# Rotary embedding, split halves: three in-place slabs of four batches in place of five of two

## The chip, the cores and the metric

One core of one Trainium2 chip. The metric is the device time of one execution in microseconds (us), of which the profiled span (first to last instruction) is about 1.8 us less. The kernel before takes 163.34 us (median of four runs, 163.23 to 163.87). Runs are marked fast or slow; a run counts as slow when it is over 1.5% above the fastest run of the same kernel in the same session.

Names used below: PE (TensorE) does the matmuls, DVE (VectorE) and ACT (ScalarE) work element by element, POOL is GpSimd, SP (SyncE) here only issues DMAs. SBUF is the on-chip memory, PSUM the memory that PE writes. A cast here turns float32 into bf16; an eviction copies a result from PSUM to SBUF.

## The reference, cut to what matters

```python
batch, seq, dim, num_heads = 16, 512, 1024, 16     # x is float32, 33.6 MB
x = x.reshape(batch, seq, num_heads, 64)
x1, x2 = x[..., :32], x[..., 32:]
# cos, sin: [512, 32] float32, the same for every batch and head
rotated = np.concatenate([x1 * cos - x2 * sin,
                          x1 * sin + x2 * cos], axis=-1)      # float32, 33.6 MB
```

## The kernel before

The input is cut into eight slabs of two batches (4.2 MB). A slab is [128 partitions, 8192 floats]: each partition holds eight consecutive sequence positions, so that a DMA moves 128 rows of 32 KB. Results overwrite the slab in place, and the slab is stored from there. Five slabs fit; load 5 takes the buffer of slab 0 and waits until store 0 has landed.

```python
nb, slots, lead, rows = 2, 5, 5, 2          # cut: shapes
def load(s):
    slab[s] = slabs.tile([P, W], f32, tag="slab", name="slab")
    nc.sync.dma_start(out=slab[s], in_=dram(x, s))          # issued from SP
for s in range(lead): load(s)
# cut: cos and sin go by 64 rows of 1 KB into SBUF and by matmul to all partitions
for s in range(nslabs):
    xs = slab.pop(s)
    for k in range(rpp // rows):
        xk = view(xs, k * PW, (1, PW))                      # 2048 columns
        nc.scalar.copy(out=xb, in_=xk)                      # ACT: cast to bf16
        nc.vector.tensor_mul(out=t1, in0=xb, in1=tab(cc))   # DVE: two products
        nc.vector.tensor_mul(out=t2, in0=xb, in1=tab(ss))
        # cut: per bank of 512, PE adds t1 and the half-swapped t2 (identity weights)
        nc.scalar.copy(out=xk, in_=acc)                     # ACT: eviction, in place
    nc.scalar.dma_start(out=dram(out_flat, s), in_=xs)      # store, issued from ACT
    if s + lead < nslabs: load(s + lead)
```

A scheduler orders each engine's instructions when the kernel is built, so that the order on an engine is not the order of this text. It places casts of the next slab ahead of the last evictions and of the store of the current one.

Of the kernel before, what the change touches and what calls it, by code (L numbers as in the profile page):

```python
# [2 lines left out]

# [4 lines left out]


@with_exitstack  # L10
def kernel(
    ctx: ExitStack,
    tc: tile.TileContext,
    x: bass.AP,
    cos: bass.AP,
    sin: bass.AP,
    num_heads: int,
    out: bass.AP,
):
    nc = tc.nc  # L20
    P = nc.NUM_PARTITIONS

    batch, seq, dim = x.shape
    nh = num_heads
    hd = dim // nh
    half = hd // 2
    bf16 = mybir.dt.bfloat16
    f32 = mybir.dt.float32

    nb = 2  # L30
    slots = 5
    lead = 5
    nslabs = batch // nb
    rpp = nb * seq // P
    W = rpp * dim
    SP = seq // rpp
    rows = 2
    PW = rows * dim
    BANK = 512
    hpb = BANK // hd  # L40

    out_flat = out.rearrange("b s h d -> b s (h d)")

    singles = ctx.enter_context(tc.tile_pool(name="singles", bufs=1))
    slabs = ctx.enter_context(tc.tile_pool(name="slabs", bufs=slots))
    tpool = ctx.enter_context(tc.tile_pool(name="tpool", bufs=3))
    psum = ctx.enter_context(tc.tile_pool(
        name="psum", bufs=2, space=bass.MemoryType.PSUM))


    def dram(t, s):
        return bass.AP(tensor=t.tensor, offset=t.offset + s * nb * seq * dim,
                       ap=[[W, P], [1, W]])


    def view(t, offset, *dims):
        return dataclasses.replace(t, offset=t.offset + offset,
                                   ap=[t.ap[0], *[list(d) for d in dims]])


    slab = {}


    def load(s):
        slab[s] = slabs.tile([P, W], f32, tag="slab", name="slab")
        nc.sync.dma_start(out=slab[s], in_=dram(x, s))


    for s in range(lead):
        load(s)  # L70



    cos_sb = singles.tile([SP, rpp * half], f32, tag="cos_sb")
    sin_sb = singles.tile([SP, rpp * half], f32, tag="sin_sb")
    for t, src in ((cos_sb, cos), (sin_sb, sin)):
        nc.scalar.dma_start(out=t, in_=bass.AP(  # L77
            tensor=src.tensor, offset=src.offset,
            ap=[[rpp * half, SP], [1, rpp * half]]))

    ident = singles.tile([P, P], bf16, tag="ident")
    masks.make_identity(nc, ident)
    spread = singles.tile([SP, P], bf16, tag="spread")
    for g in range(P // SP):
        nc.gpsimd.tensor_copy(out=spread[:, g * SP:(g + 1) * SP],  # L85
                              in_=ident[:SP, :SP])


    cc1 = singles.tile([SP, rpp * hd], bf16, tag="cc1")
    ss1 = singles.tile([SP, rpp * hd], bf16, tag="ss1")  # L90
    nc.vector.tensor_copy(  # L91
        out=cc1, in_=view(cos_sb, 0, (half, rpp), (0, 2), (1, half)))
    sin_rows = view(sin_sb, 0, (half, rpp), (1, half))
    nc.vector.tensor_copy(  # L94
        out=view(ss1, 0, (hd, rpp), (1, half)), in_=sin_rows)
    nc.vector.tensor_scalar_mul(  # L96
        out=view(ss1, half, (hd, rpp), (1, half)), in0=sin_rows, scalar1=-1.0)
    cc = singles.tile([P, rpp * hd], bf16, tag="cc")
    ss = singles.tile([P, rpp * hd], bf16, tag="ss")
    for wide, one in ((cc, cc1), (ss, ss1)):  # L100
        acc = psum.tile([P, PW], f32, tag="acc", name="acc")
        for q in range(0, rpp * hd, BANK):
            n = min(BANK, rpp * hd - q)
            nc.tensor.matmul(view(acc, q, (1, n)), spread, view(one, q, (1, n)),  # L104
                             start=True, stop=True)
        nc.vector.tensor_copy(out=wide, in_=view(acc, 0, (1, rpp * hd)))  # L106

    for s in range(nslabs):
        xs = slab.pop(s)
        for k in range(rpp // rows):  # L110
            xk = view(xs, k * PW, (1, PW))
            xb = tpool.tile([P, PW], bf16, tag="xb")
            t1 = tpool.tile([P, PW], bf16, tag="t1")
            t2 = tpool.tile([P, PW], bf16, tag="t2")
            nc.scalar.copy(out=xb, in_=xk)  # L115

            def tab(t):
                return view(t, k * rows * hd, (hd, rows), (0, nh), (1, hd))

            nc.vector.tensor_mul(out=t1, in0=xb, in1=tab(cc))  # L120
            nc.vector.tensor_mul(out=t2, in0=xb, in1=tab(ss))  # L121
            acc = psum.tile([P, PW], f32, tag="acc")
            for q in range(0, PW, BANK):
                bank = view(acc, q, (1, BANK))
                nc.tensor.matmul(bank, ident, view(t1, q, (1, BANK)),  # L125
                                 start=True, stop=False)
                nc.tensor.matmul(  # L127
                    bank, ident,
                    view(t2, q + half, (hd, hpb), (-half, 2), (1, half)),
                    start=False, stop=True)  # L130

            nc.scalar.copy(out=xk, in_=acc)  # L132
        nc.scalar.dma_start(out=dram(out_flat, s), in_=xs)
        if s + lead < nslabs:
            load(s + lead)


# [1 line left out]
_INS = ['x', 'cos', 'sin', 'num_heads']  # L139
_OUTS = [((16, 512, 16, 64), 'float32')]  # L140

_NUMBERS = {'num_heads': 16}


# [26 lines left out]
```

## Time and profile before

| | kernel before |
|---|---|
| time, us | 163.34 |
| span of the profiled run, us | 161.5 |
| DMA packet time (two queues' shares x span), us | 97.3% x 161.5 = 157.1 |
| busy: ACT, PE, DVE, us | 117.2, 79.1, 76.4 |

From the page of the kernel before: the span; busy time by engine; the busy tenths and rate of DMA in 40 slices; the queues (q1 loads, q10 stores and tables; the last number is the share of 16 engines' span that their packets took); the costliest groups (operation, out<-in, count, busy us, mean ns); and the DMA issues.

```profile
span 161.5 us, 816 instructions
PE 79.1 (49%) x258; PEld 28.6 (18%) x258; DVE 76.4 (47%) x69; ACT 117.2 (73%) x65; POOL 1.1 (1%) x8
...
DMA  7999999999999999999999999999999999997996
...
q1 hardware_dynamic: 1152, 33.55, 48.9%
q10 hardware_dynamic: 1312, 33.69, 48.4%
...
L115 ACT CAST xb<-slab 128x2048 bf16<-128x2048 f32 x32 | 59.6, 1905 | 19.1 <-DMA slab<-in_x_dram 16.6
L120 DVE TENSOR_TENSOR t<-xb,cc 128x2048 bf16<-128x2048 bf16 x32 | 39.1, 1222 | 51.5 <-ACT xb L115 51.5
...
slab<-in_x_dram SPq DMA_DIRECT2D x8, 4096.0 KB, 29.6
out_dram<-slab ACTq DMA_DIRECT2D x8, 4096.0 KB, 25.5
```

The row of DMA digits says it all: nearly every slice is 9. The engines' waits (ACT is idle for 44 of 161.5 us) cost nothing while DMA has queued work. The one soft spot is near the end. From the windows view of the same kernel (stretch and its length in us; busy time and instruction count of PE, PE's weight loads, DVE, ACT and POOL; granted clock; DMA share; GB/s):

```profile
147.00:148.00 1.00, 0.43 (x3) 0.00 (x0) 0.00 (x0) 1.00 (x2) 0.00 (x0) 1.00 1.14 492
148.00:149.00 1.00, 0.00 (x0) 0.00 (x0) 0.00 (x0) 1.00 (x1) 0.00 (x0) 1.00 0.23 98
149.00:150.00 1.00, 0.00 (x0) 0.00 (x0) 0.00 (x0) 0.43 (x1) 0.00 (x0) 1.00 0.08 33
150.00:151.00 1.00, 0.00 (x0) 0.00 (x0) 0.00 (x0) 0.00 (x0) 0.00 (x0) 1.00 1.22 524
```

Here the queued stores are done and the last slab's own store waits for its last eviction. A packet is put down to the stretch in which it starts, so that the rate is rough. By the trace's DMA records (start, duration and size of each packet), at least half of the 16 engines are idle from 149.0 to 150.4 us, and at no other time between 1.9 us and the last packets at 160.1 us for longer than 0.5 us.

### The profile page before, as it was taken

How to read it: one execution, taken by the hardware profiler on the slowest of the kernel's cores; microseconds unless marked ns; L12 is line 12 of the kernel's file. 1: busy time of each engine (PE TensorE's matmuls, PEld its weight loads, DVE VectorE, ACT ScalarE, POOL GpSimd, SP SyncE). 2: the span in 40 equal slices, each digit the busy share in tenths (PEclk: the TensorE clock that was granted, in tenths of full speed). 3: DMA queues.
4: the chain of work that ended last, by engine and by line, in shares of the span. 5: the costliest groups of instructions: out<-in, count | busy, mean ns of one | idle time of the engine just before them, and what ended most of it. 6: DMA issues, size and time to landing. Idle time of an engine off the chain costs nothing.

```text
span 161.5 us, 816 instructions
## 1 busy us (share of the span) xinstructions
PE 79.1 (49%) x258; PEld 28.6 (18%) x258; DVE 76.4 (47%) x69; ACT 117.2 (73%) x65; POOL 1.1 (1%) x8
## 2 busy tenths in 40 slices
PE   0001189646069754932995288079754278085000
PEld 0000023212013221310341033023321022021000
DVE  0000699065099429707955484299335172280000
ACT  3006647994999999899989998969990697918000
POOL 2000000000000000000000000000000000000000
PEclk9999999999858998796599969957999557659855
DMA  7999999999999999999999999999999999997996
GB/s 260 398 398 406 422 487 389 414 495 389 389 503 406 389 495 410 389 503 406 391 495 406 400 487 414 398 479 422 398 479 418 389 487 422 398 479 316 389 389 260
DMA packets 2468, 67.29 MB, mean 417 GB/s; under 512 B 288, under 2 KB 416, under 8 KB 416
## 3 DMA queue, kind: packets, MB, share of 16 engines
q1 hardware_dynamic: 1152, 33.55, 48.9%
q10 hardware_dynamic: 1312, 33.69, 48.4%
q8 instruction: 2, 0.03, 0.1%
q14 instruction: 2, 0.02, 0.0%
HBM read 33.69 MB, written 33.55 MB: 416 GB/s over the span
## 4 chain that ended last, share of the span: by engine, by line
DMA 46%; PE 17%; ACT 14%; issue 9%; DVE 6%; ACTq 0%; DVEq 0%; SPq 0%
DMA out_dram<-slab 18%; DMA slab<-in_x_dram 18%; DMA sin_sb<-in_sin_dram 10%; PE acc L127 9%; ACT slab L132 8%; PE acc L125 7%; ACT xb L115 6%; DVE t L121 5%; DVE t L120 1%; PE acc L104 0%; ACTq L77 0%; DVE ss L94 0%; DVE ss L96 0%; DVEq L120 0%; ACTq L132 0%
## 5 line engine op out<-in xcount | busy, mean ns | idle before, releaser
L125 PE MATMUL acc<-t,ident 128*128 128x512 bf16 x128 | 58.8, 459 | 43.6 <-DVE t L120 33.3
L115 ACT CAST xb<-slab 128x2048 bf16<-128x2048 f32 x32 | 59.6, 1905 | 19.1 <-DMA slab<-in_x_dram 16.6
L132 ACT COPY slab<-acc 128x2048 f32<-128x2048 f32 x32 | 59.2, 1870 | 11.1 <-PE acc L127 10.6
L120 DVE TENSOR_TENSOR t<-xb,cc 128x2048 bf16<-128x2048 bf16 x32 | 39.1, 1222 | 51.5 <-ACT xb L115 51.5
L127 PE MATMUL acc<-t,ident 128*128 128x512 bf16 x128 | 57.9, 452 | 7.5 <-DVE t L121 7.3
L121 DVE TENSOR_TENSOR t<-xb,ss 128x2048 bf16<-128x2048 bf16 x32 | 39.0, 1219 | 0.0
L127 PEld LDWEIGHTS <-ident 128*128 128x128 bf16 x128 | 14.3, 112 | 58.8 <-issue 50.6
L125 PEld LDWEIGHTS <-ident 128*128 128x128 bf16 x128 | 14.1, 110 | 47.1 <-issue 28.7
L104 PE MATMUL acc<-cc,spread 64*128 64x512 bf16 x1 | 0.6, 582 | 12.5 <-DVE cc L91 12.5
L91 DVE CAST cc<-cos_sb 64x512 bf16<-64x512 f32 x1 | 0.4, 419 | 12.1 <-DMA cos_sb<-in_cos_dram 12.1
L104 PE MATMUL acc<-ss,spread 64*128 64x512 bf16 x1 | 0.6, 582 | 4.7 <-DVE ss L96 4.7
L115 ACT ACT_TABLE_LOAD x1 | 1.3, 1283 | 2.0 <-issue 2.0
L94 DVE CAST ss<-sin_sb 64x256 bf16<-64x256 f32 x1 | 0.3, 286 | 4.8 <-DMA sin_sb<-in_sin_dram 4.8
L104 PEld LDWEIGHTS <-spread 64*128 64x128 bf16 x2 | 0.2, 100 | 12.4 <-issue 10.6
L106 DVE CAST ss<-acc 128x512 bf16<-128x512 f32 x1 | 0.7, 692 | 0.1
L106 DVE CAST cc<-acc 128x512 bf16<-128x512 f32 x1 | 0.7, 676 | 0.0
L85 POOL COPY spread<-ident 64x64 bf16<-64x64 bf16 x2 | 0.4, 229 | 0.1
masks.py:199 POOL TENSOR_SCALAR_AFFINE_SELECT ident<-ident 128x128 bf16<-128x128 bf16 x1 | 0.3, 293 | 0.1
L96 DVE TENSOR_SCALAR ss<-sin_sb 64x256 bf16<-64x256 f32 x1 | 0.3, 278 | 0.0
masks.py:197 POOL MEMSET ident<- 128x128 bf16 x1 | 0.2, 204 | 0.3 <-POOLq L152 0.3
L152 POOL MEMSET const-bfloat16-1.0<- 128x1 bf16 x1 | 0.1, 101 | 0.0
L152 POOL MEMSET const-uint8-127<- 128x1 uint8 x1 | 0.1, 101 | 0.0
(2 smaller groups left out, 0.2 us busy)
## 6 DMA issues: line engine op xcount, KB each, us to landing
slab<-in_x_dram SPq DMA_DIRECT2D x8, 4096.0 KB, 29.6
out_dram<-slab ACTq DMA_DIRECT2D x8, 4096.0 KB, 25.5
cos_sb<-in_cos_dram ACTq DMA_DIRECT2D x1, 64.0 KB, 11.3
sin_sb<-in_sin_dram ACTq DMA_DIRECT2D x1, 64.0 KB, 16.0
```

The costliest lines, as they stand in the source:

```text
L85: nc.gpsimd.tensor_copy(out=spread[:, g * SP:(g + 1) * SP], in_=ident[:SP, :SP])
L91: nc.vector.tensor_copy(out=cc1, in_=view(cos_sb, 0, (half, rpp), (0, 2), (1, half)))
L94: nc.vector.tensor_copy(out=view(ss1, 0, (hd, rpp), (1, half)), in_=sin_rows)
L96: nc.vector.tensor_scalar_mul(out=view(ss1, half, (hd, rpp), (1, half)), in0=sin_rows, scalar1=-1.0)
L104: nc.tensor.matmul(view(acc, q, (1, n)), spread, view(one, q, (1, n)), start=True, stop=True)
L106: nc.vector.tensor_copy(out=wide, in_=view(acc, 0, (1, rpp * hd)))
L115: nc.scalar.copy(out=xb, in_=xk)
L120: nc.vector.tensor_mul(out=t1, in0=xb, in1=tab(cc))
L121: nc.vector.tensor_mul(out=t2, in0=xb, in1=tab(ss))
L125: nc.tensor.matmul(bank, ident, view(t1, q, (1, BANK)), start=True, stop=False)
L127: nc.tensor.matmul(bank, ident, view(t2, q + half, (hd, hpb), (-half, 2), (1, half)), start=False, stop=True)
L132: nc.scalar.copy(out=xk, in_=acc)
```

## The change

The intent: fewer, larger transfers (rows of 64 KB); tables that land sooner, by 16 rows each in place of 64; one product instruction in place of two per operand (on rows half as wide, so that there are 64 of them before and after); a quarter of the evictions moved from ACT to DVE; and a shorter tail, by storing the last slab in four parts.

```diff
-    nb = 2
-    slots = 5
-    lead = 5
+    nb = 4
+    slots = 3
-    rows = 2
+    rows = 1
     # cut: tpool has 2 buffers, PSUM 4 of [128, 1024]; the tables come as 16 rows
     #      of 4 KB, issued after load 0, and stand once, as cos | sin
-            nc.vector.tensor_mul(out=t1, in0=xb, in1=tab(cc))
-            nc.vector.tensor_mul(out=t2, in0=xb, in1=tab(ss))
+                nc.vector.tensor_mul(                     # 2048 results from 1024 columns
+                    out=view(t, j * dim, (PW, 2), (half, 2 * nh), (1, half)),
+                    in0=view(xb, j * dim, (0, 2), (half, 2 * nh), (1, half)),
+                    in1=view(tab, (k * rows + j) * half,
+                             (TW, 2), (0, 2 * nh), (1, half)))
     # cut: three matmuls a bank (512, 256 and 256 columns, the last with -identity)
-            nc.scalar.copy(out=xk, in_=acc)
-        nc.scalar.dma_start(out=dram(out_flat, s), in_=xs)
+            if k % 4 == 3:
+                nc.vector.tensor_copy(out=xk, in_=acc)
+            else:
+                nc.scalar.copy(out=xk, in_=acc)
+            part = rpp // rows // 4
+            if s == nslabs - 1 and k % part == part - 1:
+                a = (k + 1 - part) * PW
+                nc.scalar.dma_start(out=dram(out_flat, s, a, part * PW),
+                                    in_=view(xs, a, (1, part * PW)))
+        if s < nslabs - 1:
+            nc.scalar.dma_start(out=dram(out_flat, s), in_=xs)
```

Four slabs remain, 0 to 3, and three fit. Load 3 waits until store 0 has landed.

More of the change, by code (lines that the diff above doesn't have):

```diff
@@ L45, with dram @@
     slabs = ctx.enter_context(tc.tile_pool(name="slabs", bufs=slots))
-    tpool = ctx.enter_context(tc.tile_pool(name="tpool", bufs=3))
+    tpool = ctx.enter_context(tc.tile_pool(name="tpool", bufs=2))
     psum = ctx.enter_context(tc.tile_pool(
-        name="psum", bufs=2, space=bass.MemoryType.PSUM))
-    def dram(t, s):
-        return bass.AP(tensor=t.tensor, offset=t.offset + s * nb * seq * dim,
-                       ap=[[W, P], [1, W]])
+        name="psum", bufs=8 * BANK // PW, space=bass.MemoryType.PSUM))
+    def dram(t, s, a=0, n=W):
+        return bass.AP(tensor=t.tensor, offset=t.offset + s * nb * seq * dim + a,
+                       ap=[[W, P], [1, n]])
     def view(t, offset, *dims):
@@ L66, in load @@
         nc.sync.dma_start(out=slab[s], in_=dram(x, s))
-    for s in range(lead):
-        load(s)
-    cos_sb = singles.tile([SP, rpp * half], f32, tag="cos_sb")
-    sin_sb = singles.tile([SP, rpp * half], f32, tag="sin_sb")
-    for t, src in ((cos_sb, cos), (sin_sb, sin)):
-        nc.scalar.dma_start(out=t, in_=bass.AP(
-            tensor=src.tensor, offset=src.offset,
-            ap=[[rpp * half, SP], [1, rpp * half]]))
+    load(0)
+    TP = 16
+    PS = P // TP
+    TR = seq // TP
+    G = TR // rpp
@@ new lines @@
+    TW = rpp * half
+    tab1 = tpool.tile([P, 2 * TR * half], bf16, tag="t", name="tab1")
+    for i, src in enumerate((cos, sin)):
+        raw = tpool.tile([P, TR * half], f32, tag="t", name="raw")
+        nc.vector.memset(raw, 0.0)
+        nc.scalar.dma_start(out=raw[::PS, :], in_=bass.AP(
+            tensor=src.tensor, offset=src.offset,
+            ap=[[TR * half, TP], [1, TR * half]]))
+        nc.vector.tensor_copy(
+            out=view(tab1, i * TW, (2 * TW, G), (1, TW)),
+            in_=view(raw, 0, (TW, G), (1, TW)))
@@ L81 @@
+    for s in range(1, slots):
+        load(s)
     ident = singles.tile([P, P], bf16, tag="ident")
     masks.make_identity(nc, ident)
-    spread = singles.tile([SP, P], bf16, tag="spread")
-    for g in range(P // SP):
-        nc.gpsimd.tensor_copy(out=spread[:, g * SP:(g + 1) * SP],
-                              in_=ident[:SP, :SP])
-    cc1 = singles.tile([SP, rpp * hd], bf16, tag="cc1")
-    ss1 = singles.tile([SP, rpp * hd], bf16, tag="ss1")
-    nc.vector.tensor_copy(
-        out=cc1, in_=view(cos_sb, 0, (half, rpp), (0, 2), (1, half)))
@@ L93 @@
-    sin_rows = view(sin_sb, 0, (half, rpp), (1, half))
-    nc.vector.tensor_copy(
-        out=view(ss1, 0, (hd, rpp), (1, half)), in_=sin_rows)
-    nc.vector.tensor_scalar_mul(
-        out=view(ss1, half, (hd, rpp), (1, half)), in0=sin_rows, scalar1=-1.0)
-    cc = singles.tile([P, rpp * hd], bf16, tag="cc")
-    ss = singles.tile([P, rpp * hd], bf16, tag="ss")
-    for wide, one in ((cc, cc1), (ss, ss1)):
-        acc = psum.tile([P, PW], f32, tag="acc", name="acc")
-        for q in range(0, rpp * hd, BANK):
-            n = min(BANK, rpp * hd - q)
-            nc.tensor.matmul(view(acc, q, (1, n)), spread, view(one, q, (1, n)),
-                             start=True, stop=True)
-        nc.vector.tensor_copy(out=wide, in_=view(acc, 0, (1, rpp * hd)))
+    minus = singles.tile([P, P], bf16, tag="minus")
@@ new lines @@
+    nc.gpsimd.memset(minus, 0.0)
+    nc.gpsimd.affine_select(
+        out=minus, in_=minus, compare_op=mybir.AluOpType.not_equal, fill=-1.0,
+        base=0, pattern=[[-1, P]], channel_multiplier=1)
+    spread = singles.tile([P, G * P], bf16, tag="spread")
+    nc.gpsimd.memset(spread, 0.0)
+    for g in range(G):
+        part = view(spread, g * P + g, (SP, P // SP), (G, TP))
+        nc.gpsimd.affine_select(
+            out=part, in_=part, compare_op=mybir.AluOpType.not_equal, fill=1.0,
+            base=0, pattern=[[0, P // SP], [-PS, TP]], channel_multiplier=1)
@@ new lines @@
+    tab = singles.tile([P, 2 * TW], bf16, tag="tab")
+    for a in range(0, 2 * TW, PW):
+        acc = psum.tile([P, PW], f32, tag="acc", name="acc")
+        n = min(PW, 2 * TW - a)
+        for q in range(0, n, BANK):
+            m = min(BANK, n - q)
+            for g in range(G):
+                nc.tensor.matmul(view(acc, q, (1, m)),
+                                 view(spread, g * P, (1, P)),
+                                 view(tab1, g * 2 * TW + a + q, (1, m)),
+                                 start=g == 0, stop=g == G - 1)
+        nc.vector.tensor_copy(out=view(tab, a, (1, n)), in_=view(acc, 0, (1, n)))
@@ L112 @@
             xb = tpool.tile([P, PW], bf16, tag="xb")
-            t1 = tpool.tile([P, PW], bf16, tag="t1")
-            t2 = tpool.tile([P, PW], bf16, tag="t2")
+            t = tpool.tile([P, 2 * PW], bf16, tag="t")
             nc.scalar.copy(out=xb, in_=xk)
-            def tab(t):
-                return view(t, k * rows * hd, (hd, rows), (0, nh), (1, hd))
-            nc.vector.tensor_mul(out=t1, in0=xb, in1=tab(cc))
-            nc.vector.tensor_mul(out=t2, in0=xb, in1=tab(ss))
+            for j in range(rows):
+                nc.vector.tensor_mul(
[3 more added lines that the diff above has]
+                             (TW, 2), (0, 2 * nh), (1, half)))
@@ L122 @@
             acc = psum.tile([P, PW], f32, tag="acc")
             for q in range(0, PW, BANK):
-                bank = view(acc, q, (1, BANK))
-                nc.tensor.matmul(bank, ident, view(t1, q, (1, BANK)),
-                                 start=True, stop=False)
-                nc.tensor.matmul(
-                    bank, ident,
-                    view(t2, q + half, (hd, hpb), (-half, 2), (1, half)),
-                    start=False, stop=True)
-            nc.scalar.copy(out=xk, in_=acc)
@@ L133 @@
-        nc.scalar.dma_start(out=dram(out_flat, s), in_=xs)
-        if s + lead < nslabs:
-            load(s + lead)
+                nc.tensor.matmul(view(acc, q, (1, BANK)), ident,
+                                 view(t, q, (1, BANK)), start=True, stop=False)
+                nc.tensor.matmul(view(acc, q + half, (hd, hpb), (1, half)), ident,
+                                 view(t, PW + q, (hd, hpb), (1, half)),
+                                 start=False, stop=False)
+                nc.tensor.matmul(view(acc, q, (hd, hpb), (1, half)), minus,
+                                 view(t, PW + q + half, (hd, hpb), (1, half)),
+                                 start=False, stop=True)
@@ L139 @@
+        if s + slots < nslabs:
+            load(s + slots)
 _INS = ['x', 'cos', 'sin', 'num_heads']
```

## The prediction

> **What bounds the kernel now.** The DMA engines. In the queue table the load queue holds 48.9% and the store queue 48.4% of 16 engines' span: 97.3% of 161.5 us, or 157 us for 67.3 MB, 428 GB/s. The Trainium skill, "DMA: Bandwidth & Descriptors", Specifications, puts the fabric ceiling at 435 GB/s: 1 to 2% left. By the windows only three stretches are poor: the first 2 us, 148 to 150 us (33 to 98 GB/s, between the last queued store and the last slab's own store, issued at 149.5), and the last 2 us. ACT is busy 117 us, PE 79, DVE 76: their waits are hidden while transfers are queued.
>
> **What the change saves.** At most about 4 us of gaps. Larger rows save nearly nothing: 1024 packets of 32 KB already take 1.23 us each on the load queue (0.489 x 161.5 x 16 / 1024). The tables (sin lands at 17.3 us) leave the path, since slab 0 now lands only at about 22 us. ACT loses a quarter of its evictions to DVE. DVE product time (1.2 us per 2048 elements) and PE columns are unchanged.
>
> **What it costs.** An 8.4 MB transfer takes about 19.5 us alone. Load 3 waits for store 0, with little queued work to hide anything. The program order on ACT matters most: each store is issued from ACT *behind* three casts of the next slab, so store 2 cannot be issued before load 3 has landed, even when slab 2 is long computed.
>
> My sum, an estimate from the trace's durations (ACT 1024 columns about 0.95 us, from 1.80 per 2048; DVE product 1.15 to 1.22, DVE eviction 1.2; PE 0.95 to 1.7 us per 1024 outputs, as matmuls of 512 columns take 0.22 or 0.43 us in the chain):
> - Loads 0 to 2 and store 0 (issued near 53) are four transfers: store 0 lands near 80. Load 3 is issued near 81; store 1 near 82 to 86. About 3 us of DMA idle.
> - Load 3 and store 1 share the engines (same page, Queues, rings and completion order: round-robin between rows; the 389 to 503 GB/s slices before show no penalty). Both land near 117 to 121.
> - Casts of slab 3 start, then store 2 is issued near 123 to 126: 4 to 6 us of DMA idle.
> - In slab 3 the order on ACT becomes three evictions, then four casts, with two xb buffers: a round trip of cast, two products, DVE eviction, two products, PE, ACT eviction, about 9.5 us per four rows, 38 to 40 us for the slab. The last quarter is issued near 162, after DMA has run dry again, and lands about 6.5 us later: span near 169.5.
>
> The measured time exceeds the span by 1.8 us: **171.3 us**, 4.9% slower. Range 165.5 to 178. Chances: faster 0.05, same 0.12, slower 0.83.
>
> **What would show each step.** Groups: ACT casts about 1.05 us, DVE product about 1.2 us. Chain: load 3, then slab 3's ACT/DVE/PE round trips, then a 2 MB store. Waits: ACT's cast on load 3 of several us; SP's load 3 on store 0 from about 3 to 80 us. Windows: DMA near 432 GB/s to 80, idle near 82 and 122, and holes between the last stores.
>
> **What would make it wrong.** If PE stays at 0.43 us per 512 columns through slabs 2 and 3, over 178. If the product slows with its 32-element runs (DVE then 2 us per row), far over 178. If slab 3 overlaps better than my round trip, or store 1 comes late and load 3 lands earlier, towards 164.

## The result, and the profile after

The changed kernel takes 177.47 us (median of four fast runs, 176.57 to 178.34). The ratio to the kernel before is 1.086 (95% interval 1.080 to 1.092). Ratios here are the mean time of one kernel's fast runs over that of the other's of the same rounds, so not quite the ratio of the medians quoted.

From the page of the changed kernel, the lines that answer to those of before:

```profile
span 174.8 us, 1125 instructions
PE 81.4 (47%) x388; PEld 43.1 (25%) x388; DVE 98.3 (56%) x85; ACT 110.0 (63%) x113; POOL 1.8 (1%) x11
...
DMA  7996999969999699992999979999195997998355
...
q1 hardware_dynamic: 576, 33.55, 46.0%
q10 hardware_dynamic: 1072, 33.69, 44.9%
...
L131 DVE TENSOR_TENSOR t<-xb,tab 128x2048 bf16<-128x2048 bf16 x64 | 76.3, 1221 | 44.3 <-ACT xb L128 41.0
L128 ACT CAST xb<-slab 128x1024 bf16<-128x1024 f32 x64 | 65.5, 1050 | 25.2 <-DMA slab<-in_x_dram 22.1
...
out_dram<-slab ACTq DMA_DIRECT2D x4, 2048.0 KB, 9.7
slab<-in_x_dram SPq DMA_DIRECT2D x4, 41.3
```

The row of DMA digits now has holes: the 2 in the middle, the 1 after it, the 3 near the end. The packets' time is nearly the same, 90.9% of 174.8 = 158.9 us against 157.1. So the transfers are hardly slower; the engines stand idle between them. By the DMA records at least half of them are idle from 81.1 to 84.3, 124.5 to 128.5 and 163.2 to 168.4 us: 12.4 us in sum against 1.4 before. That is 11.0 of the 13.3 us by which the span grew; the 1.8 us of packet time are most of the rest. The windows view of the changed kernel, in these stretches:

```profile
81.10:84.30 3.20, 2.02 (x12) 1.12 (x12) 2.60 (x3) 3.20 (x4) 0.00 (x0) 1.00 0.50 164
124.50:128.50 4.00, 1.87 (x6) 0.86 (x6) 3.30 (x3) 3.59 (x5) 0.00 (x0) 0.50 0.04 16
163.20:168.40 5.20, 1.86 (x6) 0.69 (x5) 2.27 (x2) 0.00 (x0) 0.00 (x0) 0.50 0.07 28
```

What ends each hole is read from the timeline of the ACT engine (start us, duration us, instruction, count; in brackets the idle time before it and what ended it; ACTq lines are DMA issues):

```profile
84.15 0.34 ACTq L157 DMA_DIRECT2D out_dram<-slab  x1
...
124.13 1.04 ACT L128 CAST xb<-slab 128x1024 bf16<-128x1024 f32 x1 [13.37 <-DMA slab<-in_x_dram]
125.08 1.01 ACT L150 COPY slab<-acc 128x1024 f32<-128x1024 f32 x1
125.98 1.99 ACT L128 CAST xb<-slab 128x1024 bf16<-128x1024 f32 x2
127.65 0.34 ACTq L157 DMA_DIRECT2D out_dram<-slab  x1
128.38 1.01 ACT L150 COPY slab<-acc 128x1024 f32<-128x1024 f32 x1 [0.41 <-PE acc L143]
130.71 1.01 ACT L150 COPY slab<-acc 128x1024 f32<-128x1024 f32 x1 [1.31 <-PE acc L143]
132.41 1.01 ACT L150 COPY slab<-acc 128x1024 f32<-128x1024 f32 x1 [0.69 <-PE acc L143]
133.32 1.99 ACT L128 CAST xb<-slab 128x1024 bf16<-128x1024 f32 x2
135.66 2.18 ACT L128 CAST xb<-slab 128x1024 bf16<-128x1024 f32 x2 [0.35 <-DVE t L131]
138.84 0.34 ACTq L154 DMA_DIRECT2D out_dram<-slab  x1
...
167.51 0.34 ACTq L154 DMA_DIRECT2D out_dram<-slab  x1
```

Read it from the top. ACT stands still for 13.37 us, with slab 2's remaining work behind it, because the cast that is next in its order needs load 3, and load 3 had to wait for store 0. The waits of SP, which issues the loads, show that (us in total, times, longest):

```profile
SPq L65 <- DMA out_dram<-slab: 59.5, 1, 59.5
```

Only then does the last ACT eviction of slab 2 run (125.08) and store 2 go out (127.65). That is the second hole. Then the four parts of slab 3 come at 138.84, 148.39, 157.39 and 167.51, slower than DMA drains them. That is the third hole. The first hole lies before load 3 and store 1: store 0 has drained, load 3 is issued only when it has landed, and store 1 is issued at 84.15.

### The profile page after: what moved, and what is told of

Same layout as the page of the kernel before. It is cut to its first block, busy times and chain, and to the rows that moved or that the text cites. A ratio compares the mean times of both kernels' runs of the same rounds, so it can differ in the third digit from the quotient of the medians.

```text
span 174.8 us, 1125 instructions
## 1 busy us (share of the span) xinstructions
PE 81.4 (47%) x388; PEld 43.1 (25%) x388; DVE 98.3 (56%) x85; ACT 110.0 (63%) x113; POOL 1.8 (1%) x11
## 4 chain that ended last, share of the span: by engine, by line
DMA 36%; ACT 22%; DVE 18%; PE 15%; issue 4%; ACTq 0%; DVEq 0%
DMA slab<-in_x_dram 36%; DVE t L131 13%; ACT xb L128 13%; ACT slab L150 9%; PE acc L138 8%; DVE slab L148 5%; PE acc L143 3%; PE acc L140 3%; ACTq L150 0%; DVEq L148 0%; DVEq L131 0%; ACTq L128 0%
## 5 line engine op out<-in xcount | busy, mean ns | idle before, releaser
L131 DVE TENSOR_TENSOR t<-xb,tab 128x2048 bf16<-128x2048 bf16 x64 | 76.3, 1221 | 44.3 <-ACT xb L128 41.0
L138 PE MATMUL acc<-t,ident 128*128 128x512 bf16 x128 | 57.5, 449 | 63.7 <-DVE t L131 62.4
L128 ACT CAST xb<-slab 128x1024 bf16<-128x1024 f32 x64 | 65.5, 1050 | 25.2 <-DMA slab<-in_x_dram 22.1
L150 ACT COPY slab<-acc 128x1024 f32<-128x1024 f32 x48 | 48.5, 1014 | 14.2 <-PE acc L143 13.5
L143 PE MATMUL acc<-t,minus 128*128 128x256 bf16 x128 | 40.2, 314 | 0.0
L140 PE MATMUL acc<-t,ident 128*128 128x256 bf16 x128 | 40.1, 313 | 0.0
L148 DVE COPY slab<-acc 128x1024 f32<-128x1024 f32 x16 | 19.5, 1221 | 4.9 <-PE acc L143 4.9
L143 PEld LDWEIGHTS <-minus 128*128 128x128 bf16 x128 | 14.3, 112 | 21.1 <-issue 10.7
L116 PE MATMUL acc<-tab,spread 128*128 128x512 bf16 x4 | 2.0, 608 | 21.0 <-DVE tab L84 21.0
L80 DVE MEMSET raw<- 128x1024 f32 x2 | 1.8, 912 | 1.3 <-PEq L176 1.0
```

The lines of the kernel that those rows point to most:

```text
L80: nc.vector.memset(raw, 0.0)
L116: nc.tensor.matmul(view(acc, q, (1, m)), view(spread, g * P, (1, P)), view(tab1, g * 2 * TW + a + q, (1, m)), start=g == 0, stop=g == G - 1)
L131: nc.vector.tensor_mul(out=view(t, j * dim, (PW, 2), (half, 2 * nh), (1, half)), in0=view(xb, j * dim, (0, 2), (half, 2 * nh), (1, half)), ...
L138: nc.tensor.matmul(view(acc, q, (1, BANK)), ident, view(t, q, (1, BANK)), start=True, stop=False)
L140: nc.tensor.matmul(view(acc, q + half, (hd, hpb), (1, half)), ident, view(t, PW + q, (hd, hpb), (1, half)), start=False, stop=False)
L143: nc.tensor.matmul(view(acc, q, (hd, hpb), (1, half)), minus, view(t, PW + q + half, (hd, hpb), (1, half)), start=False, stop=True)
```

## The experiments

Theory, called the chain: load 3 waits for store 0; slab 3's compute waits for load 3; store 2 waits behind slab 3's casts; the last quarter's store waits for slab 3's slow alternation. Rivals: large rows or large transfers cost by themselves; the new form of compute (twice as many casts and evictions, three matmuls a bank, runs of 32 elements) costs; or every hole in DMA is simply time to be taken back one by one. All outputs were correct.

### e1: slab 3's casts behind store 2

```diff
-            nc.scalar.copy(out=xb, in_=xk)
+            with tc.issue_after(held) if s == nslabs - 1 else ExitStack():   # order on ACT only
+                nc.scalar.copy(out=xb, in_=xk)
-            nc.scalar.dma_start(out=dram(out_flat, s), in_=xs)
+            held = nc.scalar.dma_start(out=dram(out_flat, s), in_=xs).ins
```

> Slab 3's casts stand behind store 2 in ACT's order, nothing else is changed. Chain theory (load 3 lands near 124 us, then slab 3's round trips of about 10 us per four rows, then the last quarter's store): store 2 is issued near 111 us instead of 127.65, the DMA hole at 124.5 to 128.5 us goes, but load 3 and slab 3's round trips stay, so the hole before the last quarter grows by as much: 175 to 179 us, within 2% of the changed kernel. Rival, every DMA hole is simply lost time and can be taken back one by one: the 4.0 us come back, 173.5 us.

Measured: one fast run of 169.22 us and three of 172.15 to 173.54 that count as slow, so no interval. Against my expectation this gained. As it gave no interval, it was run again:

> The same kernel as e1, whose runs were spread from 169.2 to 173.5 us, again for an interval. New theory (after e1 to e3): in the changed kernel slab 2's leftovers, an eviction on ACT, one on DVE and the store's issue, stand behind the wait for load 3 and lengthen slab 3's first four rows from about 9.5 to 14.7 us; e1 takes them out, so 4.5 to 8 us come off: 169.5 to 173 us, first four rows about 9.7 us, slab 3 about 39 us. First theory (nothing gained): 175 us or more.

Measured: 172.87 us (median of five fast runs of 171.44 to 173.99; a sixth of 175.85 counts as slow; ratio to before 1.056, interval 1.052 to 1.061). The changed kernel's ratio was 1.086, so the edit gives back some 3%, about 5 us. (Over both sessions this one kernel ranges from 169.2 to 175.9 us, so its size is the least certain here.) The rival's number (173.5) was the better one; the next two runs tell whether its reason was.

### e2: the last slab's parts issued from SP; e3: both

```diff
-                nc.scalar.dma_start(out=dram(out_flat, s, a, part * PW),
+                nc.sync.dma_start(out=dram(out_flat, s, a, part * PW),
```

> The four part stores of the last slab are issued from SP instead of ACT; the scheduler then keeps casts and evictions of slab 3 alternating on ACT. Chain theory: slab 3's compute falls from 43 us (124.1 to 167.5) to about 30, the last part waits for the DMA queue and not for compute, the hole of 5.2 us before 168.4 goes: stores run without a break from 128.5 us, 38.8 us for 16.8 MB, span near 169, 170.8 us measured (169.5 to 172.5). Rival, large descriptors or the transfers themselves are slow: no change, 177 us.

> e1 and e2 together. Chain theory: now nothing is behind load 3's wait and slab 3 computes in about 30 us from 124; DMA runs without a break from 84.3 us on: load 3 and store 1 to about 124, store 2 to 143.5, store 3 to 163, so a span near 165 and 166.5 us measured (165.5 to 168); only the hole at 81 to 84 us is left. If holes add up one by one whatever the chain, e3 gains the sum of what e1 and e2 gain; in the chain theory it gains some 4 us more than e2 although e1 alone gains nothing.

Measured: e2 173.15 us (median of three fast runs, 173.03 to 173.57; a fourth of 175.92 counts as slow; ratio 1.059, 1.054 to 1.064); e3 168.31 us (four fast runs, 167.85 to 169.06, ratio 1.029, 1.024 to 1.034). Both are about 2 us above what was expected; the order is right. But the test for e3 went to the rival: by the ratios e1 gives back 4.8 us, e2 4.4 and both together 9.3, which is as good as their sum. The third hole is gone in e2; in e3 only the first is left (81.3 to 84.6 us).

Slab 3's compute, from its first cast to the end of the issue of its last part, in fast profiled runs, and its first four rows, from the first cast to the issue of the first part:

| | parts issued from ACT | parts issued from SP |
|---|---|---|
| casts ahead of store 2 | changed kernel: 43.7 us, first four rows 14.7 | e2: 34.2 us, 14.8 |
| casts behind store 2 | e1 again: 41.0 us, 10.2 | e3: 29.3 us, 9.3 |

Both edits shorten the work in slab 3. The parts on ACT cost 9.5 to 12 us: each issue stands in ACT's order until the group's last eviction is done, and the scheduler then puts three evictions and four casts in a row, where they alternate in e2 and e3. Slab 2's leftovers cost about 5 us in the first four rows. From the ACT timeline of e3, beside that of the changed kernel above:

```profile
126.92 1.99 ACT L129 CAST xb<-slab 128x1024 bf16<-128x1024 f32 x2 [14.56 <-DMA slab<-in_x_dram]
129.25 2.18 ACT L129 CAST xb<-slab 128x1024 bf16<-128x1024 f32 x2 [0.34 <-DVE t L132]
131.34 1.01 ACT L151 COPY slab<-acc 128x1024 f32<-128x1024 f32 x1
132.50 1.04 ACT L129 CAST xb<-slab 128x1024 bf16<-128x1024 f32 x1 [0.16 <-DVE t L132]
```

In e3 four casts come in the first 4.5 us. In the changed kernel the fourth comes 9.2 us after the first, behind slab 2's eviction, the issue and three evictions that each wait for PE. So e1 takes work out of the chain itself, and I read the rival's number as having come out for another reason than the rival's. That is read from single profiled runs and is not all of it: e1 again issued its last part 5.1 us before the changed kernel (162.38 against 167.51), of which 2.7 us are the shorter slab 3 and 2.4 us a load 3 that came earlier (first cast at 121.77 against 124.13; in e2 124.55, in e3 126.92). Why load 3 came earlier was not tested. In e2 the chain no longer ends last: DMA runs without a break from 129.0 us, and store 2 and the four parts, 16.8 MB, set the end. That is why e2 gains less than the 9.5 us by which slab 3 shortened. It is also why, from e2 to e3, closing the second hole (3.9 us in e2's records) is worth its full length: 4.8 us come off. A hole is slack only while something else ends last.

### e4: small slabs, everything else as changed

```diff
-    nb = 4
-    slots = 3
+    nb = 2
+    slots = 5
```

> The slab size alone is undone: two batches a slab, five slots, everything else as changed (rows of 1024, one product operation, quarter of the evictions on DVE, 16-descriptor tables, four part stores). Chain theory: loads always have a free slot or queued stores beside them, DMA stays busy, 161.5 to 164 us. Rival, the new compute (more and smaller instructions, three matmuls per bank, 32-element runs) is what costs: 170 us or more.

Measured: 166.29 us (median of three fast runs, 165.65 to 167.86; ratio 1.018, interval 1.010 to 1.026: not clear of 2%). Undoing the slab size gives back some 11 of the 14 us, so it is the main cause; but this is about 2 us more than the top of the range expected. The records show where it lies in the profiled run (167.86 us, the longest of the three): holes from 156.3 to 158.2 us (the last quarter, behind ACT's order, again), and from 160.7 us on one DMA engine alone runs on to 164.6, the other 15 being done.

### e8: small slabs, six slots, parts from SP

```diff
-    nb = 4
-    slots = 3
+    nb = 2
+    slots = 6
-                nc.scalar.dma_start(out=dram(out_flat, s, a, part * PW),
+                nc.sync.dma_start(out=dram(out_flat, s, a, part * PW),
```

> Two batches a slab with six slots (the same bytes as three of four), the last slab's four parts issued from SP, compute as changed. Chain theory: the end of e4 (ACT's order in the last slab, holes from 156 to 158 us) goes: 163 to 165 us. One DMA engine that lags the others at the end (in e4 it alone ran 3.9 us longer) may keep it there rather than at 162; if that lag is what the e4 loss was and it stays, 165 to 166.

Measured: two fast runs, 163.68 and 164.08 us, and two slow ones of 173 and 174. Repeated for an interval:

> The same kernel as e8, which had two fast runs of four, again for an interval: fast runs 163.5 to 164.3 us, level with the kernel before.

Measured: three fast runs of 163.91 to 164.57 us, ratio 1.003 (1.000 to 1.007); three slow ones of 173 to 174 again. In its fast runs the new compute form (rows of 1024, three matmuls a bank, the new tables) is level with the kernel before. So it is not what the loss was. (e8 changes two things against e4, the slots and the issuing engine; which of them took off the last 2 us was not separated.) Half of this kernel's runs are slow, which no run of the kernel before was; why is open.

### e5: large slabs, most of the rest as in the kernel before

The old tables do not fit beside three large slabs (by my note), so that the new tables stay. So do the rows of 1024 columns, the three matmuls a bank and the buffers; the expectation names the tables alone.

```diff
-    # one tensor_mul of (PW, 2) products; evictions with k % 4 == 3 on DVE; four part stores
+    # two tensor_mul of PW each; all evictions on ACT; one store per slab
```

> Only the large slabs (and the tables, which do not fit in their old form beside three slabs) are kept: two separate products, all evictions on ACT, one store for the last slab as in the kernel before. Chain theory: large slabs alone make the loss, and the rest of the change softens it: load 3 lands near 115 to 120, slab 3 runs from about 122 to 157, its one 8.4 MB store then has the engines to itself: 182 us (179 to 187), slower than the changed kernel. Rival, the new compute form is a good part of the loss: below 174 us.

Measured: 179.82 us (179.23 to 180.86, ratio 1.099, 1.093 to 1.105). With the product form, the DVE evictions and the part stores undone, the loss is still there, and larger. As e8 has what stays here at no loss, large slabs stored and loaded whole are enough for it. The records show DMA idle from 145.9 to 158.2 us, before the last slab's one store.

### e6: one store for the last slab

```diff
-            if s == nslabs - 1 and k % part == part - 1:      # four part stores
-                ...
-        if s < nslabs - 1:
-            nc.scalar.dma_start(out=dram(out_flat, s), in_=xs)
+        nc.scalar.dma_start(out=dram(out_flat, s), in_=xs)
```

> The changed kernel with the last slab stored by one DMA. Chain theory: slab 3 computes faster (its order on ACT is not cut by DMA issues: last eviction near 158 instead of 167), but then 8.4 MB are still to be stored with nothing beside them, 19.4 us + 1 to 2: span about 180, 182 us measured (179 to 185): the four parts gain about 5 us. Rival, the part stores cost as much through ACT's order as they save: 177 us.

Measured: two fast runs, 179.15 and 181.79 us (ratio 1.103, 1.091 to 1.114), two slow ones of 184.60 and 191.04. So the four parts seem to gain about 3 us (1.086 against 1.103, with intervals that just overlap; I had expected 5), although their place on ACT makes slab 3 slower: in this kernel slab 3 took 33.6 us (122.42 to 155.98), and the store then had DMA to itself.

### e7: store 0 and load 3 in halves; e9: stores 1 and 2 too

Both start from e3. Load 3 writes into the same buffer object as slab 0, so that its first half waits for the first half of store 0 alone; store 0's halves are issued from SP.

```diff
+        slab[s] = held_slab[s - slots]                        # load 3: slab 0's buffer
+        for a in (0, W // 2):
+            nc.sync.dma_start(out=view(slab[s], a, (1, W // 2)),
+                              in_=dram(x, s, a, W // 2))
-            part = rpp // rows // 4
-            if s == nslabs - 1 and k % part == part - 1:
+            part = rpp // rows // (2 if s == 0 else 4)
+            if s in (0, nslabs - 1) and k % part == part - 1:
```

> e3 with store 0 and load 3 in two halves each, so that the first half of load 3 waits for the first half of store 0 alone (same buffer, the wait is by region). Chain theory: the hole at 81 to 84 us goes, load 3's first half lands near 96 and slab 3 waits for no load; DMA is the bound again: span 161 to 163, 163 to 165 us measured, level with the kernel before although the slabs are large. If the large slabs or 64 KB rows cost by themselves: 168 us as e3.

Measured: two fast runs of 167.90 and 168.44 us (ratio 1.027, 1.021 to 1.034) and two slow ones of 172.04 and 180.16. The time is that of e3. The only profile is of the slow run of 172.04 us, so what follows is how that run went, and no size of the fast runs is read from it. In it the first hole is gone, but ACT waits for load 3's second half, which was issued at 86:

```profile
146.27 1.04 ACT L136 CAST xb<-slab 128x1024 bf16<-128x1024 f32 x1 [15.46 <-DMA slab<-in_x_dram]
```

The DMA view of e7 from 88 to 108 us (queue: packets, MB, share; q1 loads, q10 stores):

```profile
q10 hardware_dynamic: 91, 5.96, 71.4%
q1 hardware_dynamic: 88, 2.56, 29.6%
```

and of the changed kernel in the same stretch:

```profile
q10 hardware_dynamic: 64, 4.19, 48.5%
q1 hardware_dynamic: 63, 4.13, 47.6%
```

The two queues take turns by packet, and in the records a data packet is one partition's row. Halving load 3 made its rows 32 KB beside stores of 64 KB: nearly as many packets (10 of the 88 are completion packets of 4 bytes, so 78 rows beside 91), under half the bytes. The Trainium skill, "DMA: Bandwidth & Descriptors", Queues, rings and completion order, says that each engine goes round the queues packet by packet; the trace agrees, with 91 packets against 88 (64 against 63 in the changed kernel). If this was what held e7 back, halving stores 1 and 2 as well must end it:

```diff
-            held = nc.scalar.dma_start(out=dram(out_flat, s), in_=xs).ins
+            for a in (0, W // 2):
+                held = nc.scalar.dma_start(out=dram(out_flat, s, a, W // 2),
+                                           in_=view(xs, a, (1, W // 2))).ins
```

> e7, with stores 1 and 2 in two halves too, so that both queues carry rows of 32 KB. In e7 load 3's second half landed only at 144 us, beside stores with rows of 64 KB. Theory, sharing goes by packet and not by byte, so that half rows got a third of the rate beside whole rows: now load 3's second half lands near 120 to 126 us, slab 3 does not wait for it for more than a few us, the holes after 145 us shrink to under 3 us in sum: span 161 to 164, 163 to 166 us measured. Rival, load 3 was late in e7 because its second half was issued late behind store 0 on the same queue: it lands near 144 again and the time stays near 168.

Measured: 164.03 us (four fast runs, 163.85 to 164.31; ratio 1.003, 0.999 to 1.007). The same view of e9, 88 to 108 us:

```profile
q10 hardware_dynamic: 151, 4.42, 51.4%
q1 hardware_dynamic: 146, 4.26, 49.3%
```

The bytes are level again, and no hole is left before the end. Load 3's second half landed later than I had put it, but nothing came of that:

```profile
133.49 1.04 ACT L136 CAST xb<-slab 128x1024 bf16<-128x1024 f32 x1 [5.14 <-DMA slab<-in_x_dram]
```

It was issued at 95, 9 us later than in e7 (whose last packet of load 3 ended at 145.8, not at the 144 of the expectation), and still its first cast came 13 us earlier. So it was not the late issue, the rival of the expectation, that held e7 back. With the holes closed, large slabs cost nothing (1.003); at 164.03 us this still does not beat the kernel before. (e9 also lets the first halves of stores 1 and 2 go out before their slab is done, which e7 does not; so the sharing is shown by the views, and its cost of 4 us only together with that.)

### b1: the kernel before, with its last slab stored in parts from SP

```diff
             nc.scalar.copy(out=xk, in_=acc)
-        nc.scalar.dma_start(out=dram(out_flat, s), in_=xs)
+            if s == nslabs - 1:
+                nc.sync.dma_start(out=dram(out_flat, s, k * PW, PW), in_=xk)
+        if s < nslabs - 1:
+            nc.scalar.dma_start(out=dram(out_flat, s), in_=xs)
```

> The kernel before with the last slab's store in four parts issued from SP, nothing else. The only hole in its DMA, 149.0 to 150.4 us, should go: 1.4 us, 162.0 us against 163.5. If one lagging DMA engine (which catches up in that hole) then ends last, the gain is under 1 us, 162.5 to 163.5.

Measured: 163.46 us (six fast runs, 163.28 to 163.57; ratio 0.999, 0.996 to 1.002). The hole at 149 us is gone and the gain is nothing. By the records, the packets of the kernel before end within 0.2 us of each other at 160.0 to 160.2; in b1 the engines finish from 158.6 to 160.1. In the kernel before, the last rows of the queued stores end from 148.6 to 150.35 us, and the last slab's store starts on all engines at 150.3 to 150.45: the hole was time in which the late engines caught up. In b1 they stay 1.5 us apart to the end. The last DMA engine ends at the same time either way. No version here beats the kernel before.

## Why the prediction was right or wrong

- **What bounds the kernel before: right.** DMA, with one hole of 1.4 us. b1 adds that even this hole was not to be had; my "at most about 4 us" of savings was too generous.
- **Larger rows save nothing: right.** In the DMA records a row of 32 KB took 1213 ns on its engine at the median (432 GB/s for 16), one of 64 KB 2418 to 2421. The skill's rule on the same page (Rules for kernel authors: 128 partitions and at least 1 MiB a DMA for the best rate) was met by 4.2 MB already, and going to 8.4 MB gained nothing.
- **The product operation costs nothing: right.** It took 1221 ns for 2048 results with 32-element runs, 1222 before with 64. The skill, "VectorE: DVE Perf Modes", Side-by-side: where the cycles go for N=2048 bf16, gives about 1224 ns for 2048 elements in its two-per-cycle mode, so that the short runs keep this mode. DVE's 22 us more are its 16 evictions (19.5 us) and the table work. The evictions are not off the path: by the page of the changed kernel they are 5% of the chain that ended last, as the prediction had them in its round trip.
- **The tables: right that they are off the path, but the change did not bring them sooner.** The second table landed at 21.2 us (issued at 13.09, 8.1 us to landing) against 17.3 before, because it waits for a buffer that the first one uses. Slab 0 came at 23.6, so that it did not matter.
- **The first two holes: right.** Predicted: about 3 us near 82 and 4 to 6 near 122. Measured: 3.2 at 81.1 and 4.0 at 124.5.
- **Slab 3: mechanism right, size off.** Predicted: about 9.5 us per four rows, "38 to 40 us for the slab", last quarter issued "near 162". Measured: 14.7, 9.6, 9.0 and 10.1 us between issues, 43.7 in all, and the last issue at 167.5. The term that was mis-sized is the first group of four rows: I counted slab 2's leftovers as the cause of a late store 2 only, and not as work that stands between slab 3's own casts. e2 against e3 shows it: 14.8 against 9.3 us. These 5 us are nearly all of the 5.3 by which the span was missed (169.5 against 174.8). Load 3 landed at about 124, past my 117 to 121; that added little, for 162 less 38 to 40 us puts the start of slab 3 in my sum at 122 to 124.
- **The total: right side, inside the range, at its upper end.** 177.47 against 171.3 (165.5 to 178): a loss of 14.1 us where 8.0 were forecast, and one of the four runs (178.34) lies above the range. The profiled run itself was the fastest of the four (176.57).
- **My expectation for e1 was wrong**, for the same reason: I took the second hole to be slack and did not see that slab 2's leftovers behind it lengthen slab 3.

## What to carry to other kernels

When DMA is busy throughout and larger rows move at the same rate (1213 ns for 32 KB, 2418 to 2421 for 64 KB here), a change to transfer size or compute can gain no more than DMA's holes, and even a hole may only be waiting for the slowest DMA engine; what can be lost is the queued work that hides everything else. That goes with how finely buffers are filled and released, not with their total size: six small slabs (e8, in its fast runs) and three large ones moved in halves (e9) were level with the kernel before, while the same bytes in three slabs, moved whole but for the last store, lost 8.6%, and still 2.9% with ACT's order mended (e3). A DMA issue on a compute engine is an instruction in that engine's order: see what stands ahead of it (here a cast that waits for a load) and what it holds up behind it. When two queues compete, compare the sizes of their rows: they take turns by row, and halving one side's rows took its share of the bytes from half to 30% (profiled run of e7).

## What the Trainium skill lacked or had wrong

- "DMA: Bandwidth & Descriptors" says that queues take turns by packet, but not what that does to unequal rows: with rows of 32 KB against 64 KB the queues had 88 and 91 packets, and 2.56 and 5.96 MB (e7). It puts a packet at about 9 to 17 descriptors; here the trace records a whole row of 32 or 64 KB as one packet, and does not say how many descriptors that is.
- The same page notes that engines 7 and 15 are usually slower, with a guess that it ties to DMAs issued from GpSimd, but gives no size and nothing for DMAs issued from SP and ACT, as all of x and out are here. One engine ended up to 3.9 us after the others (e4), and 1.5 us after the first in b1, where that ate the whole gain of a closed hole. The records used here do not name the engine, and what makes it late was not tested.
- No page that I read for this says that a DMA issue placed on a compute engine breaks that engine's alternation: issuing four part stores from SP in place of ACT took 9.5 us off slab 3 (43.7 to 34.2 us, e2). The order on ACT was the build's scheduler's, so this is shown for its order alone.
